# Five buffers for each split part of the weights, fewer raw buffers, and a tighter layout of all stages

## The chip, the cores and the metric

The kernel runs on one core of one Trainium2 chip. The metric is the device time of one execution in microseconds (us). Engines are named as in the profile: PE is TensorE's matmul side, PEld its weight loads, DVE is VectorE, ACT is ScalarE, POOL is GpSimd, SP is SyncE, whose queue issues most loads and stores.

## The reference, cut to what matters

One block of a network on 1,024 tokens of width 1,024, in float32: two branches (a gated MLP with causal mixing inside chunks of 128 tokens, and a state-space branch with a convolution and a scan over chunks), merged by gates, then a layer norm, then an expert layer that picks 128 of 16,384 experts per token.

```python
ya = gmlp_branch(uv, ...) @ gm_w_out
yb = ssd_branch(z, xbc, dt_raw, ...) @ ssd_w_out
merged = gates[..., 0, :] * ya + gates[..., 1, :] * yb
x1 = layer_norm(DEEPNORM_ALPHA * x + merged @ w_o, ...)
ch = peer(x1, ...)          # top 16 of 16x16 sums per head, 8 heads
ple = sigmoid(x1 @ ple_w_gate + ple_b_gate) * (p @ ple_w_proj)
x = layer_norm(DEEPNORM_ALPHA * x1 + ch + ple, ...)
# in peer, for the chosen experts eb and gates gb:
act = gelu(einsum('tkd,td->tk', u_tab[eb], xb))
out = einsum('tk,tkd->td', gb * act, v_tab[eb])
```

## The kernel before, in words

The tokens are worked in three groups of 2, 3 and 3 blocks of 128 (`GROUPS`, line 22). `front(gi)` runs the dense part of a group: the gated MLP (lines 239 to 350), the state-space branch (`conv`, `make_bc`, `make_x`, `core_g`, `core`, lines 364 to 507), the merge (509 to 527), the output product with the layer norm and the side product `ple` (530 to 645), and the scores for the experts (588 to 607). In the first two groups the chosen experts' rows are gathered by POOL (`gather`, line 800) and multiplied on DVE (`experts_u`, line 822) or on PE (`experts_v`, line 864); this gather work of a group runs beside the front of the later groups. The third group computes all experts densely (`dense_scores`, `dense_gates`, `dense`, lines 908 to 1020).

Every float32 product is made of three products of rounded halves (`mm3`, line 150). So each weight slice of 512 KB is loaded by SP into a buffer `raw`, cast by ACT into `whi` (line 146), and subtracted by DVE into `wlo` (line 147): a split. Then come 24 matmuls over it (18 in the second product of the dense stage). `weights` (line 138) holds 4 `raw`, 3 `whi` and 3 `wlo` buffers, which all weights share. The tokens xT are loaded and split in `prepare` (line 203) through 4 buffers of their own.

A scheduler sets the order on each engine: it takes the instructions in program order, by priority, and `tc.high_priority(offset=n)` moves what stands inside n places ahead. Each engine then works in that order and waits by semaphores for buffers and data.

In `dense`, `gte` (line 973) holds the gates for GI = 4 slices of 128 experts, read from DRAM in runs of GI*TC*4 = 512 bytes; `ewh`, `ewl` hold finished pieces, 13 of each. The output products land in 4 PSUM buffers `po`, of which a half step uses 3, and DVE adds them to `eacc` (line 1013).

```python
raw = wp.tile([128, k, n], F32, name="raw", tag="raw", bufs=4)
hi = wp.tile([128, k, n], F32R, name="whi", tag="whi", bufs=3)
lo = wp.tile([128, k, n], F32R, name="wlo", tag="wlo", bufs=3)
with tc.high_priority(offset=AHEAD_W[0]):
    DMA.dma_start(raw, src)
with tc.high_priority(offset=AHEAD_W[1]):
    A.copy(hi, raw)
    V.tensor_sub(lo, raw, hi.bitcast(F32))
```

Of the kernel before, what the change touches and what calls it, by code (L numbers as in the profile page):

```python
# [8 lines left out]
F32 = mybir.dt.float32  # L9
# [15 lines left out]
TC, GI = 32, 4  # L25
# [16 lines left out]
AHEAD_W = (20, 20)  # L42
# [36 lines left out]
def block_kernel(ctx, tc, a, out):  # L79
# [119 lines left out]
    def prepare(gi):  # L199
# [8 lines left out]
        with tc.tile_pool(name="xr", bufs=4, side=where) as xr:  # L208
            for k in range(KD):
                raw = xr.tile([128, T], F32, name="xraw")  # L210
                DMA.dma_start(raw, a["xT"][:, k, t0:t0 + T])
                split(xh[:, k], xl[:, k], raw)
        tokens[gi] = es, xp, xh, xl

    def front(gi):
# [24 lines left out]
        with tc.tile_pool(name="ga", bufs=1, side=side_) as ga, \  # L240
                tc.tile_pool(name="gb", bufs=2, side=side_) as gb:

            wst = ga.tile([128, 8, 128], F32, name="wst")
            DMA.dma_start(wst, a["wst"])
            add = ga.tile([128, 8, 128], F32, name="add")
            DMA.dma_start(add, rows(a["gmbs"], 0, 1024))
            V.tensor_mul(wst, wst, tri[:, None, :].to_broadcast([128, 8, 128]))
# [10 lines left out]
            with tc.tile_pool(name="sd", bufs=1, side=side_) as sd:  # L258
                raw = wp.tile([128, KD, NCOL], F32, name="raw", tag="raw", bufs=4)
                DMA.dma_start(raw, a["w_dt"])  # L260
                dh = wp.tile([128, KD, NCOL], F32R, name="whi", tag="whi", bufs=3)
                dl = wp.tile([128, KD, NCOL], F32R, name="wlo", tag="wlo", bufs=3)
                split(dh, dl, raw)
                pw = psm.tile([NCOL, T], F32, name="mm")
                for k in range(KD):
                    mm3(pw, (dh[:, k], dl[:, k]), (xh[:, k], xl[:, k]), k == 0, k == KD - 1)
                dtw = gb.tile([NCOL, T], F32, name="dtw", tag="t1", bufs=3)
                A.copy(dtw, pw)
                pd = pst.tile([128, NB, NCOL], F32, name="mt", tag="mt")
                for c in range(NB):  # L270
                    PE.transpose(pd[:, c, :], dtw[:, c * 128:c * 128 + 128], ident[:NCOL, :NCOL])
                sh = [128, NB, NCOL]
                dt = xp.tile(sh, F32, name="dt")
                V.tensor_add(dt, pd, dtb[:, None, :].to_broadcast(sh))
                e = sd.tile(sh, F32, name="e")
                A.activation(e, dt, AF.Abs)
                A.activation(e, e, AF.Exp, scale=-1.0)
                r = sd.tile(sh, F32, name="r")
                V.tensor_scalar_add(r, e, 2.0)
                V.reciprocal(r, r)  # L280
                V.tensor_mul(e, e, r)
                V.tensor_mul(r, e, e)
                q = sd.tile(sh, F32, name="q")
                V.tensor_scalar_mul(q, r, 2.0 / 17)
                for n in (15, 13, 11, 9, 7, 5, 3):
                    V.scalar_tensor_tensor(q, q, 2.0 / n, r, op0=OP.add, op1=OP.mult)
                V.scalar_tensor_tensor(q, q, 2.0, e, op0=OP.add, op1=OP.mult)
                V.scalar_tensor_tensor(dt, dt, 0.0, q, op0=OP.max, op1=OP.add)
                V.tensor_mul(e, dt, nega[:, None, :].to_broadcast(sh))
                pc = pst.tile([128, 2, NB * NCOL], F32, name="mt", tag="mt")  # L290
                dtaf = e.rearrange("p c h -> p (c h)")
                PE.matmul(pc[:, 0, :], lhsT=tri, rhs=dtaf, start=True, stop=True)
                PE.matmul(pc[:, 1, :], lhsT=ones, rhs=dtaf, start=True, stop=True)
                acs = xp.tile(sh, F32, name="acs")
                acsf = acs.rearrange("p c h -> p (c h)")
                A.copy(acsf, pc[:, 0, :])
                cdec = xp.tile(sh, F32, name="cdec")
                A.activation(cdec.rearrange("p c h -> p (c h)"), pc[:, 1, :], AF.Exp)
                dtd = xp.tile(sh, F32, name="dtd")
                dtdf = dtd.rearrange("p c h -> p (c h)")  # L300
                V.tensor_sub(dtdf, pc[:, 1, :], acsf)
                A.activation(dtdf, dtdf, AF.Exp)
                V.tensor_mul(dtd, dtd, dt)
                pt = pst.tile([NB * NCOL, 128], F32, name="mt", tag="mt")
# [4 lines left out]
                for c in range(NB):  # L309
                    DMA.dma_start(arow[:, c, :], act[c * NCOL:(c + 1) * NCOL, :])  # L310
# [809 lines left out]
```

## Time and profile before

| what | value |
|---|---|
| time, median of 3 runs | 3759.26 us (3750.78 to 3759.49) |
| the profiled execution's own time | 3774.55 us |
| its span, first to last instruction | 3772.9 us |
| PE busy | 3437.7 us, 91% |
| PEld busy | 2946.2 us, 78% |
| DVE busy | 2936.8 us, 78% |
| ACT busy | 1756.0 us, 47% |
| POOL busy | 1606.3 us, 43% |
| mean granted TensorE clock | 0.955 of full |
| moved by DMA | 1183.88 MB, mean 314 GB/s |

A share of busy time is an average over the whole span. A wait in the profile is an engine's idle time, put down to whatever ended it last. Matmuls follow each other before the one ahead has ended, so PE's busy time says when it had work, not how fast it went.

### The profile page before, as it was taken

What the parts mean: (1) busy time and instruction counts of PE and PEld (TensorE: products, weight loads), DVE (VectorE), ACT (ScalarE), POOL (GpSimd) and SP (SyncE); (2) the same over time, 40 slices, a digit from 0 to 9 for tenths busy, and PEclk for the clock granted to TensorE, in tenths of its full rate; (3) what the DMA queues carried; (4) which work ended last, traced back from release to release, by engine and by line L of the source; (5) the groups of instructions that cost most, each with busy time, mean ns of one, the idle gap of its engine ahead of it and who ended that gap; (6) DMA issues with size and microseconds to landing.
All of it is one profiled execution on the core that took longest, in us unless ns stands there. A gap on an engine that the chain in (4) does not pass through costs nothing.

```text
span 3772.9 us, 59493 instructions
## 1 busy us (share of the span) xinstructions
PE 3437.7 (91%) x21390; PEld 2946.2 (78%) x21390; DVE 2936.8 (78%) x6823; ACT 1756.0 (47%) x2675; POOL 1606.3 (43%) x1310
## 2 busy tenths in 40 slices
PE   8898997999989988999988989998889989989988
PEld 8897996988877876888878888777667868667756
DVE  6677799898977989896688999997667766766535
ACT  6788543476843333466652334774222323322223
POOL 0000004756545354554354445443556565665540
PEclk9998998999999988999989999999999999999999
DMA  5453656989879886989888899999999999999992
GB/s 200 161 172 130 238 180 241 389 309 356 317 279 385 309 324 234 356 311 343 305 326 327 298 338 349 362 377 372 360 381 400 395 386 389 368 383 401 356 350 95
DMA packets 409159, 1183.88 MB, mean 314 GB/s; under 512 B 41120, under 2 KB 139424, under 8 KB 405792
## 3 DMA queue, kind: packets, MB, share of 16 engines
q0 software_dynamic: 187488, 682.71, 47.7%
q1 hardware_dynamic: 221376, 497.38, 36.9%
q8 instruction: 168, 2.75, 0.3%
q14 instruction: 127, 1.04, 0.1%
HBM read 1121.01 MB, written 58.92 MB: 313 GB/s over the span
## 4 chain that ended last, share of the span: by engine, by line
PE 33%; DVE 16%; DMA 13%; issue 4%; ACT 1%; POOL 1%; SPq 0%; DVEq 0%; ACTq 0%; POOLq 0%
PE mm L152 6%; PE mm L154 6%; PE mm L153 6%; PE pacc L864 4%; DVE row L822 3%; DVE wlo L147 3%; DMA ew<-s 3%; PE po L152 3%; DMA row<-in_peer_v_dram,idxT 3%; PE po L153 3%; PE po L154 3%; DMA raw<-in_peer_uT_dram 2%; PE mt L947 2%; DMA row<-in_peer_u_dram,idx 1%; DMA raw<-in_peer_vd_dram 1%
## 5 line engine op out<-in xcount | busy, mean ns | idle before, releaser
L146 ACT CAST whi<-raw 128x1024 fp32r<-128x1024 f32 (+1 forms) x676 | 701.1, 1041 | 1192.4 <-PE mm L153 612.0
L803 POOL DMA_INDIRECT row<-in_peer_u_dram,idx x640 | 811.5, 1268 | 874.9 <-PE pacc L864 254.3
L147 DVE TENSOR_TENSOR wlo<-raw,whi 128x1024 fp32r<-128x1024 f32 (+1 forms) x676 | 816.2, 1210 | 375.5 <-ACT whi L146 374.7
L154 PE MATMUL mm<-xh,wlo 128*128 128x384 f32 (+2 forms) x3160 | 1056.4, 335 | 46.7 <-DVE wlo L147 46.7
L152 PE MATMUL mm<-xh,whi 128*128 128x384 f32 (+2 forms) x3160 | 1066.3, 338 | 34.3 <-ACT whi L146 25.6
L803 POOL DMA_INDIRECT row<-in_peer_v_dram,idxT x640 | 780.9, 1220 | 712.0 <-PE pacc L864 232.5
L153 PE MATMUL mm<-xl,whi 128*128 128x384 f32 (+2 forms) x3160 | 1051.9, 333 | 0.6 <-DVE xl L136 0.6
L822 DVE SCALAR_TENSOR_TENSOR row<-row,x1b 128x1024 f32<-128x1024 f32 x640 | 774.6, 1217 | 64.8 <-DMA row<-in_peer_u_dram,idx 58.5
L152 PEld LDWEIGHTS mm<-xh,whi 128*128 128x128 f32 (+1 forms) x3160 | 611.2, 194 | 89.7 <-ACT whi L146 46.1
L154 PEld LDWEIGHTS mm<-xh,wlo 128*128 128x128 f32 (+1 forms) x3160 | 609.8, 193 | 66.4 <-DVE wlo L147 55.0
L153 PEld LDWEIGHTS mm<-xl,whi 128*128 128x128 f32 (+1 forms) x3160 | 610.5, 193 | 12.2 <-issue 6.1
L864 PE MATMUL pacc<-row,zw 128*32 128x512 f32 x2560 | 316.9, 614 | 37.0 <-DMA row<-in_peer_v_dram,idxT 36.8
L152 PE MATMUL po<-whi,ewh 128*128 128x512 f32 x768 | 316.0, 411 | 32.2 <-DVE eacc L1013 32.2
L153 PE MATMUL po<-wlo,ewh 128*128 128x512 f32 x768 | 311.0, 405 | 14.4 <-DVE wlo L147 14.3
L154 PE MATMUL po<-whi,ewl 128*128 128x512 f32 x768 | 309.9, 404 | 0.0
L152 PEld LDWEIGHTS po<-whi,ewh 128*128 128x128 f32 x768 | 148.3, 193 | 104.6 <-DVE eacc L1013 36.1
L864 PEld LDWEIGHTS pacc<-row,zw 128*32 128x32 f32 x2560 | 67.9, 111 | 180.6 <-issue 131.1
L135 ACT CAST ewh<-ew 128x384 fp32r<-128x384 f32 x128 | 65.6, 514 | 296.7 <-DVE ew L985 230.1
L818 POOL DMA_DIRECT2D x1b<-x x5 | 3.0, 601 | 446.4 <-DMA x<-x 446.4
L153 PEld LDWEIGHTS po<-wlo,ewh 128*128 128x128 f32 x768 | 148.5, 193 | 51.0 <-DVE wlo L147 16.8
L154 PEld LDWEIGHTS po<-whi,ewl 128*128 128x128 f32 x768 | 148.1, 193 | 40.9 <-issue 5.0
L153 PE MATMUL mm<-wlo,xh 128*128 128x256 f32 x512 | 147.8, 289 | 11.4 <-DVE wlo L147 11.4
(272 smaller groups left out, 5603.8 us busy)
## 6 DMA issues: line engine op xcount, KB each, us to landing
raw<-in_peer_uT_dram SPq DMA_DIRECT2D x128, 512.0 KB, 8.0
raw<-in_peer_vd_dram SPq DMA_DIRECT2D x128, 512.0 KB, 6.8
raw<-in_w_xbc_dram SPq DMA_DIRECT2D x96, 512.0 KB, 5.9
raw<-in_w_g_dram SPq DMA_DIRECT2D x48, 512.0 KB, 6.7
raw<-in_w_z_dram SPq DMA_DIRECT2D x48, 512.0 KB, 5.4
raw<-in_ssd_w_out_dram SPq DMA_DIRECT2D x48, 512.0 KB, 5.3
raw<-in_w_q_dram SPq DMA_DIRECT2D x48, 512.0 KB, 4.7
g<-gt SPq DMA_DIRECT2D x24, 1024.0 KB, 7.5
```

Of the source, the lines that this page charges most:

```text
L135: A.copy(hi, src)
L146: A.copy(hi, raw)
L147: V.tensor_sub(lo, raw, hi.bitcast(F32))
L152: PE.matmul(p, lhsT=lh, rhs=rh, start=start, stop=False, skip_group_check=skip)
L153: PE.matmul(p, lhsT=lh, rhs=rl, start=False, stop=False, skip_group_check=skip)
L154: PE.matmul(p, lhsT=ll, rhs=rh, start=False, stop=stop, skip_group_check=skip)
L803: g = POOL.indirect_dma_start(out=t, out_offset=None, in_=a[tab], in_offset=bass.IndirectOffsetOnAxis(ap=ix, axis=0))
L818: POOL.dma_start(x1, x1_d[gi, c])
L822: u = V.scalar_tensor_tensor(t, t, 1.0, x1, op0=OP.mult, op1=OP.mult, accum_out=act[:, k:k + 1])
L864: return PE.matmul(pacc[q * 32:q * 32 + 32, h * 512:h * 512 + 512], lhsT=zws[z][:, q, r % 4, :], rhs=ts[q][:, h * 512:h * 512 + 512], star ...
L947: PE.matmul(p[:, i, :], lhsT=o1, rhs=o2, start=True, stop=True)
```

## The change

`weights` gets 3 `raw`, 5 `whi` and 5 `wlo` buffers, its loads stand 150 places ahead instead of 20, and its splits 100 instead of 20. The rest makes room in SBUF: GI is 2, so `gte` is loaded 64 times in runs of 256 bytes; the finished pieces are 11 of each; xT goes through the shared `raw` buffers, two rows of blocks at a time; the mixing weights `wst` and `add` are loaded and prepared per group g (`spatial`) instead of once; small tiles share the tag `t1`; `cT` has one buffer and `make_bc` stands after `core`; `ce` is written over `arow_t`, the square over `y`, the result of `ple` over `proj`; pT goes through a gather buffer, and its split (`ph`, `pl`) stands behind the output product. Besides, the adds to `eacc` stand 40 places ahead.

```diff
-TC, GI = 32, 4
+TC, GI = 32, 2
...
-AHEAD_W = (20, 20)
+AHEAD_W = (150, 100)
+NRAW, NHI = 3, 5
...
-        raw = wp.tile([128, k, n], F32, name="raw", tag="raw", bufs=4)
-        hi = wp.tile([128, k, n], F32R, name="whi", tag="whi", bufs=3)
-        lo = wp.tile([128, k, n], F32R, name="wlo", tag="wlo", bufs=3)
+        raw = wp.tile([128, k, n], F32, name="raw", tag="raw", bufs=NRAW)
+        hi = wp.tile([128, k, n], F32R, name="whi", tag="whi", bufs=NHI)
+        lo = wp.tile([128, k, n], F32R, name="wlo", tag="wlo", bufs=NHI)
...
-        with tc.tile_pool(name="xr", bufs=4, side=where) as xr:
-            for k in range(KD):
-                raw = xr.tile([128, T], F32, name="xraw")
-                DMA.dma_start(raw, a["xT"][:, k, t0:t0 + T])
-                split(xh[:, k], xl[:, k], raw)
+        for k in range(0, KD, 2):
+            raw = wp.tile([128, 2, T], F32, name="raw", tag="raw", bufs=NRAW)
+            DMA.dma_start(raw, a["xT"][:, k:k + 2, t0:t0 + T])
+            split(xh[:, k:k + 2], xl[:, k:k + 2], raw)
...
+            def spatial(g):
+
+                w = ws[g] = gb.tile([128, 128], F32, name="wst", bufs=3)
+                add = adds[g] = gb.tile([128, 1, 128], F32, name="add", bufs=3)
+                with tc.high_priority(offset=AHEAD_W[0]):
+                    DMA.dma_start(w, a["wst"][:, g, :])
+                    DMA.dma_start(add[:, 0], rows(a["gmbs"], g * 128, 128))
+                V.tensor_mul(w, w, tri)
+                pr = pst.tile([128, 128], F32, name="mt", tag="mt")
+                PE.matmul(pr, lhsT=ones, rhs=w, start=True, stop=True)
+                V.scalar_tensor_tensor(add[:, 0], pr, gmb[:, g:g + 1], add[:, 0], op0=OP.mult, op1=OP.add)
...
-                xc = sb.tile([128, T], F32, name=name, bufs=1 if name == "bT" else 2)
+                xc = sb.tile([128, T], F32, name=name, bufs=2 if name == "xs" else 1)
...
-                if j % 2 == 1 and j < 15:
-                    yield from make_bc(j // 2 + 1)
                 if j < 15:
                     yield from make_x(j + 1)
                 if j % 2 == 0:
                     core_g(j // 2)
                 yield from core(j)
+                if j % 2 == 1 and j < 15:
+                    yield from make_bc(j // 2 + 1)
...
-            if u == 1:
-                split(ph, pl, pT)
             yield 2 * unit
         mp_es.close()
+        lp = qa_es.enter_context(tc.tile_pool(name="lp", bufs=1, side=side_))
+        ph = lp.tile([128, 2, T], F32R, name="ph")
+        pl = lp.tile([128, 2, T], F32R, name="pl")
+        split(ph, pl, pT)
...
-                ready[i2] = [eb.tile([128, T], F32R, name=n, bufs=I2B + 5) for n in ("ewh", "ewl")]
+                ready[i2] = [eb.tile([128, T], F32R, name=n, bufs=I2B + 3) for n in ("ewh", "ewl")]
...
-                        V.tensor_add(o, o, po[c])
+                        with tc.high_priority(offset=AHEAD_G):
+                            V.tensor_add(o, o, po[c])
```

The change moves instructions on every engine. Three places are shown. In a row, a line number is that of its own file, and the number in a tile's name tells one buffer use from another; a slice's cast, as `whi_7761`, and the product made with it, as `mm_7766`, lie 5 apart.

ACT, in the gated MLP of the second group, where the gates `sg` are taken from the products `mm`. Before, from the product with `whi_7679` on (the next slices in order of use are 7712, 7761, 7794, 7840, 7873):

```order
L146 CAST whi_7794<-raw_7793 128x1024
L344 ACT_TABLE_LOAD
L344 ACTIVATE sg_7709<-mm_7684,c_bgate_121 128x384
L146 CAST whi_7840<-raw_7839 128x1024
L146 CAST whi_7873<-raw_7872 128x1024
L344 ACTIVATE sg_7791<-mm_7766,c_bgate_121 128x384
```

Now, from the product with `whi_7693` on (the next slices are 7726, 7775, 7808, 7854, 7887, 7936, 7969, 8015):

```order
L147 CAST whi_7854<-raw_7853 128x1024
L750 COPY gate0_1_7633<-pr_7611 128x128
L346 ACT_TABLE_LOAD
L346 ACTIVATE sg_7723<-mm_7698,c_bgate_121 128x384
L147 CAST whi_7887<-raw_7886 128x1024
L136 CAST gh_7063<-mix_7681 128x384
L346 ACTIVATE sg_7805<-mm_7780,c_bgate_121 128x384
L147 CAST whi_7936<-raw_7935 128x1024
L147 CAST whi_7969<-raw_7968 128x1024
L147 CAST whi_8015<-raw_8014 128x1024
L346 ACTIVATE sg_7884<-mm_7859,c_bgate_121 128x384
```

When the first of these gates is taken, three casts of later slices stood ahead of it before, and four now.

SP, at the start of the kernel. Before (with the semaphores that a row waits for):

```order
1 L211 DMA xraw_150<-in_xT_dram 128x256
...
4 L211 DMA xraw_162<-in_xT_dram 128x256
5 L144 DMA raw_203<-in_w_v_dram 128x1024
6 L144 DMA raw_233<-in_w_v_dram 128x1024
7 L211 DMA xraw_166<-in_xT_dram 128x256 [waits DMAHW0_49,DVE_49]
```

Now:

```order
1 L211 DMA raw_147<-in_xT_dram 128x2x256
...
3 L211 DMA raw_155<-in_xT_dram 128x2x256
4 L313 DMA wst_523<-in_wst_dram 128x128
...
9 L314 DMA add_583<-in_gmbs_dram 128x128 [waits DMAHW0_49]
10 L211 DMA raw_159<-in_xT_dram 128x2x256 [waits DMAHW1_49,DVE_49]
11 L145 DMA raw_178<-in_w_v_dram 128x1024 [waits DMAHW2_49,DVE_49]
12 L145 DMA raw_208<-in_w_v_dram 128x1024 [waits DMAHW3_49,DVE_49]
```

The first load of weights waited for nothing before; now it stands behind all of xT and waits until DVE has split the second pair of its rows.

ACT, at the end of the merge of the second group (the casts `mh` are the merge's last results, those of 128x512 belong to `ple_w_proj`). Before:

```order
L135 CAST mh_11955<-ya_12597 128x384
L146 CAST whi_12865<-raw_12864 128x1024
L146 CAST whi_12926<-raw_12925 128x1024
L135 CAST ph_12705<-pT_12700 128x768
L146 CAST whi_12968<-raw_12967 128x1024
```

Now:

```order
L136 CAST mh_11938<-ya_12580 128x384
L147 CAST whi_12945<-raw_12944 128x1024
L147 CAST whi_13014<-raw_13013 128x1024
L147 CAST whi_13056<-raw_13055 128x1024
L147 CAST whi_13165<-raw_13164 128x512
L147 CAST whi_13196<-raw_13195 128x512
L147 CAST whi_13226<-raw_13225 128x512
L147 CAST whi_13257<-raw_13256 128x512
L136 CAST ph_13124<-row_12898 128x768
```

The cast `ph` stood in the middle of the casts for the output product before; now it stands behind the casts of the four slices that are multiplied with it.

## Rows read from the trace of the kernel before

**Rows 1.** The page, part 1: busy us, share of the span, instructions of each engine.

```profile
PE 3437.7 (91%) x21390; PEld 2946.2 (78%) x21390; DVE 2936.8 (78%) x6823; ACT 1756.0 (47%) x2675; POOL 1606.3 (43%) x1310
```

**Rows 2.** Waits of PE, whole span: waiter <- releaser: us in total, times, longest.

```profile
PE mm L154 <- DVE wlo L147: 46.7, 28, 8.5
PE mm L152 <- ACT whi L146: 39.5, 29, 8.4
PE pacc L864 <- DMA row<-in_peer_v_dram,idxT: 36.8, 13, 8.4
PE po L152 <- DVE eacc L1013: 32.2, 7, 13.5
...
PE mm L153 <- DVE wlo L147: 23.5, 9, 6.2
PE po L153 <- DVE wlo L147: 14.3, 5, 5.2
```

**Rows 3.** Windows: start:end us, PE, PEld, DVE, ACT, POOL busy, PEclk, DMA share, GB/s.

```profile
0.00:560.00 560.00, 511.70 (x4040) 491.20 (x4041) 411.27 (x1041) 381.08 (x615) 2.17 (x9) 0.95 0.53 180
560.00:735.00 175.00, 148.48 (x809) 140.69 (x808) 163.15 (x379) 61.65 (x85) 105.32 (x72) 0.92 0.81 304
735.00:1215.00 480.00, 446.28 (x2979) 393.20 (x2978) 402.76 (x762) 290.77 (x450) 251.41 (x188) 0.97 0.89 329
1215.00:1505.00 290.00, 251.81 (x1601) 215.65 (x1602) 264.24 (x944) 101.14 (x148) 130.64 (x103) 0.92 0.81 292
1505.00:2080.00 575.00, 535.35 (x3499) 472.67 (x3497) 462.00 (x842) 307.20 (x476) 275.67 (x228) 0.96 0.90 328
2080.00:2600.00 520.00, 482.04 (x3050) 417.38 (x3049) 507.59 (x1740) 282.06 (x461) 239.35 (x204) 0.98 0.92 347
2600.00:3640.00 1040.00, 952.42 (x4883) 726.19 (x4881) 663.55 (x1037) 291.10 (x393) 594.59 (x500) 0.96 1.01 382
```

**Rows 4.** Timeline of PE in the state-space branch: start us, us, operation; 18 matmuls apart.

```profile
1699.82 0.33 PE L152 MATMUL mm<-xh,whi 128*128 128x384 f32 x1
...
1702.94 0.33 PE L152 MATMUL mm<-xh,whi 128*128 128x384 f32 x1
```

**Rows 5.** Waits of PE for splits, windows 560:735, 1215:1505 and 2080:2600 us.

```profile
PE mm L154 <- DVE wlo L147: 13.4, 4, 8.5
...
PE mm L152 <- ACT whi L146: 3.9, 5, 1.0
...
PE mm L153 <- DVE wlo L147: 8.5, 2, 5.4
...
PE mm L152 <- ACT whi L146: 6.4, 6, 1.9
PE mm L154 <- DVE wlo L147: 4.6, 5, 1.3
...
PE mm L154 <- DVE wlo L147: 18.5, 13, 5.7
...
PE mm L152 <- ACT whi L146: 4.8, 7, 1.4
...
PE mm L153 <- DVE wlo L147: 2.1, 2, 1.1
```

**Rows 6.** DMA of the dense stage, 2680:3600 us: queues (packets, MB, share), one issue.

```profile
q0 software_dynamic: 64658, 235.46, 65.3%
q1 hardware_dynamic: 69428, 116.35, 35.1%
...
gte<-g SPq DMA_DIRECT2D x26, 768.0 KB, 15.2
```

**Rows 7.** Timeline of the start: start us, us, operation [idle before <-releaser].

```profile
2.67 0.91 SPq L144 DMA_DIRECT2D raw<-in_w_v_dram  x2
...
7.29 1.04 ACT L146 CAST whi<-raw 128x1024 fp32r<-128x1024 f32 x1 [2.53 <-DMA raw<-in_w_v_dram]
...
8.38 0.58 PE L152 MATMUL mm<-whi,xh 128*128 128x256 f32 x1 [8.38 <-ACT whi L146]
```

More of the change, by code (lines that the diff above doesn't have):

```diff
@@ L256, in front @@
                 yield 2 * unit
[L258 to L304, printed above, removed]
-                PE.transpose(pt, acsf, ident)
-                act = sd.tile([NB * NCOL, 128], F32, name="q")
-                A.copy(act, pt)
-                arow = dram.tile([NCOL, NB, 128], F32, name=f"arow{gi}")
-                for c in range(NB):
-                    DMA.dma_start(arow[:, c, :], act[c * NCOL:(c + 1) * NCOL, :])
@@ new lines, in front @@
+            raw = wp.tile([128, KD, NCOL], F32, name="raw", tag="raw", bufs=NRAW)
+            DMA.dma_start(raw, a["w_dt"])
+            dh = wp.tile([128, KD, NCOL], F32R, name="whi", tag="whi", bufs=NHI)
+            dl = wp.tile([128, KD, NCOL], F32R, name="wlo", tag="wlo", bufs=NHI)
+            split(dh, dl, raw)
+            pw = psm.tile([NCOL, T], F32, name="mm")
+            for k in range(KD):
+                mm3(pw, (dh[:, k], dl[:, k]), (xh[:, k], xl[:, k]), k == 0, k == KD - 1)
+            dtw = gb.tile([NCOL, T], F32, name="dtw", tag="t1", bufs=3)
@@ new lines, in front @@
+            A.copy(dtw, pw)
+            pd = pst.tile([128, NB, NCOL], F32, name="mt", tag="mt")
+            for c in range(NB):
+                PE.transpose(pd[:, c, :], dtw[:, c * 128:c * 128 + 128], ident[:NCOL, :NCOL])
+            sh = [128, NB, NCOL]
+            dt = xp.tile(sh, F32, name="dt")
+            V.tensor_add(dt, pd, dtb[:, None, :].to_broadcast(sh))
+            erq = gb.tile([128, T], F32, name="erq", tag="t1", bufs=3)
+            e, r, q = [erq[:, n * NB * NCOL:(n + 1) * NB * NCOL].rearrange("p (c h) -> p c h", c=NB) for n in range(3)]
@@ new lines, in front @@
+            A.activation(e, dt, AF.Abs)
+            A.activation(e, e, AF.Exp, scale=-1.0)
+            V.tensor_scalar_add(r, e, 2.0)
+            V.reciprocal(r, r)
+            V.tensor_mul(e, e, r)
+            V.tensor_mul(r, e, e)
+            V.tensor_scalar_mul(q, r, 2.0 / 17)
+            for n in (15, 13, 11, 9, 7, 5, 3):
+                V.scalar_tensor_tensor(q, q, 2.0 / n, r, op0=OP.add, op1=OP.mult)
+            V.scalar_tensor_tensor(q, q, 2.0, e, op0=OP.add, op1=OP.mult)
+            V.scalar_tensor_tensor(dt, dt, 0.0, q, op0=OP.max, op1=OP.add)
@@ new lines, in front @@
+            V.tensor_mul(e, dt, nega[:, None, :].to_broadcast(sh))
+            pc = pst.tile([128, 2, NB * NCOL], F32, name="mt", tag="mt")
+            dtaf = e.rearrange("p c h -> p (c h)")
+            PE.matmul(pc[:, 0, :], lhsT=tri, rhs=dtaf, start=True, stop=True)
+            PE.matmul(pc[:, 1, :], lhsT=ones, rhs=dtaf, start=True, stop=True)
+            acs = xp.tile(sh, F32, name="acs")
+            acsf = acs.rearrange("p c h -> p (c h)")
+            A.copy(acsf, pc[:, 0, :])
+            cdec = xp.tile(sh, F32, name="cdec")
@@ L312, in front @@
+            A.copy(act, pt)
+            arow = dram.tile([NCOL, NB, 128], F32, name=f"arow{gi}")
+            for c in range(NB):
+                DMA.dma_start(arow[:, c, :], act[c * NCOL:(c + 1) * NCOL, :])
             for c in range(NB):
                 normalize(v[:, c], st[:, c], gb)
-            for g4 in range(0, 8, 4):
-                pr = pst.tile([128, 4, 128], F32, name="mt", tag="mt")
-                PE.matmul(pr.rearrange("p g t -> p (g t)"), lhsT=ones,
-                          rhs=wst[:, g4:g4 + 4].rearrange("p g t -> p (g t)"), start=True, stop=True)
-                for g in range(g4, g4 + 4):
-                    V.scalar_tensor_tensor(add[:, g], pr[:, g - g4], gmb[:, g:g + 1], add[:, g],
-                                           op0=OP.mult, op1=OP.add)
+            ws, adds = {}, {}
@@ L424, in core @@
                 A.activation(dec, dec, AF.Exp, scale=-1.0)
[L425 removed]
+                ce = arow_t
                 A.activation(ce, arow_t, AF.Exp)
@@ L587, in front @@
             for u in range(16):
+                if u == 4:
+                    plb = lg
+                    DMA.dma_start(plb, rows(a["ple_b_gate"], 0, 1024))
                 p = channel_major(a["w_q"][u], xh, xl)
```

57 lines of the change are left out of this document (31 added, 26 removed).

## The prediction

> **What bounds the kernel now.** I read the page first. PE is the busiest engine, 3437.7 of 3772.9 us [rows 1], so the gain to be had is in the 335 us in which it was idle and in the time at a lower clock. Then I read who PE waited for. Splits of weights end 46.7 + 39.5 + 23.5 + 14.3 = 124.0 us of it, gathered rows 36.8 us, the adds to `eacc` 32.2 us [rows 2]. Of the first four rows one is of the dense stage alone: 14.3 us at `po`. So a third of PE's idle time hangs on the part that the change enlarges.
>
> Then the windows, because what a wait is worth depends on its stage [rows 3]. The reader should look at three columns. Where DVE has room (0 to 560, 735 to 1215, 1505 to 2080: 411 of 560, 403 of 480, 462 of 575 us), a split that is late is late by its place in the queue. In three windows DVE is nearly full (560 to 735, 1215 to 1505, 2080 to 2600): it is idle for 11.9 + 25.8 + 12.4 = 50.0 us of 985, and a split is late there because DVE has too much to do. From 2600 to 3640 the DMA share is 1.01: there the queue of loads has no room left.
>
> The granted clock is the last column read. It has two levels, 1.2 and 2.4 GHz, so a mean of 0.95 is 10% of the window at the lower one. Over the six windows before 2600 that is 56 + 28 + 29 + 46 + 46 + 21 = 226 us at 1.2 GHz, beside 224 us of idle PE (the windows less PE's busy time: 48 + 27 + 34 + 38 + 40 + 38). At half speed at most half of 226 us is lost, and in part of it PE had nothing to do; I take half of that half, 56 us. So each us of PE's waiting costs some 0.25 us more by the clock, and I multiply a wait that goes by 1.25.
>
> **The change part by part.** All sums are against the profiled execution's own 3774.55 us, which is 15 us over the median of the runs; the difference is then taken from the median, 3759.26 us.
>
> *Five split buffers, splits 100 places ahead.* The 18 matmuls between the two rows of [rows 4] take 3.12 us, 0.173 us each, so a slice of 24 is 4.2 us of PE. With three buffers the cast of slice n waits until PE has done with slice n-3; then two slices lie before its use, 8.3 us. With five it waits for n-5, and four slices lie before, 16.7 us. In the built order this holds: at ACT's gates four casts stand ahead instead of three, and over all 679 splits the number of matmuls between release and use has a median of about 95 instead of 50. A cast takes 1.04 us [rows 7] and the subtraction about as long (estimate). So what can delay a split without a stall grows from some 6 to some 14 us, more than the longest of these waits, 8.5 us [rows 2].
>
> Free windows: the 124.0 us less 62.2 us in the full windows (the sum of [rows 5]) and less 14.3 us in the dense stage leave 47.5 us; 8.4 us of them are the first wait of the kernel [rows 7] and stay. Of 39.1 us I take three quarters, 29, because a core step that PE waits for can now stand behind an earlier split; with the clock **-37 us** (bounds 0 and -49).
>
> Full windows: 62.2 us hang on splits. DVE's work in them does not change, and two more split buffers let it do only two splits beforehand, about 2.5 us per window. PE can then catch up only as far as DVE was idle, 50.0 us. I take a third, 17, with the clock **-21 us** (bounds 0 and -62). The rest of these waits will appear under another name: DVE's selection, its gather products or its norms.
>
> *Dense stage: splits and the adds 40 places ahead.* They end 14.3 + 32.2 = 46.5 us of waits [rows 2]. The DMA share is 1.01 here [rows 3], so PE made faster only waits for loads. I take a quarter, **-12 us** (bounds 0 and -58, with the clock).
>
> *GI = 2: runs of 256 bytes.* The bytes stay, the packets of `gte` double. The price is read from the queues [rows 6]: q0 moves gathered rows of 4 KB, 65.3% of 920 us for 235.46 MB, 2.55 us per MB. On q1 the 168 weight slices (88.1 MB) at that rate would take 225 of its 323 us (35.1%), which leaves 98 us for the other 28.3 MB, of which `gte` is 20.4. At the rate of q0 these would take 72. The 26 us more, put on the 26 loads of `gte`, make 1.0 us for each. If that is a fixed time per packet, twice as many packets cost 1.0 us more for each of the 32 loads before, 32 us; the lower bound is 0. If a packet of 256 bytes takes as long as one of 512, each 768 KB take 3.0 us more (20.4 MB at 2.55 is 52, with the 26 that is 78, over 26): 96 us. I take the fixed time, the nearest row, and half of it, as PE and DMA take turns as the bound in this stage: **+16 us** (0 to +96).
>
> The Trainium skill speaks against this part: "DMA: Bandwidth & Descriptors", section Specifications, asks for transfers of at least 512 B for line rate and says that below it the engine reads, modifies and writes. No row here has such runs in a loaded queue. By that page the term would be the upper bound, and the sum would be 80 us worse.
>
> *Three raw buffers.* A load can be issued once the split three slices earlier is done instead of four, one slice, 4.2 us, later against its cast. If it is late, ACT and then DVE stand behind it, but PE has four slices in hand. I cost it at 0 in the sum; the cover is the split buffers, and without it each late load costs what it is late.
>
> *Start.* The first load of weights went out at 2.67 us and its product began at 8.38 [rows 7]. Now it waits for the second pair of xT rows and stands behind ten more issues, which I put at 2 to 5 us: **+3 us**.
>
> *The cast `ph`.* It now stands directly ahead of its product in the second and third group, so PE waits there for a cast and a subtraction of 768 columns, under 1.04 us [rows 7] each: **+4 us** (0 to 4.2, less the earlier waits there).
>
> *The mixing weights in pieces.* Eight small masks and products per group for one and two large ones, 42 more small loads, behind which SP's loads stand: **+3 us** (0 to 8), on DVE in its full windows. `make_bc` after `core` with one `cT`: the same instructions, less distance from the convolution to `core_g`, more from `core` to the next; 0 (-6 to +6). The merged xT loads, `ce`, `sq` and `proj` in place, `ple`'s single buffer: 0, off the path or only tighter.
>
> Sum: -37 - 21 - 12 + 16 + 3 + 4 + 3 = **-44 us**, 3759.26 - 44 = **3715 us**.
>
> **The rivals.**
>
> *PE is freed almost everywhere.* For it: DVE's idle time would cover 50 us even in the full windows, and a fuller reserve may smooth the dense stage too. Against it: DMA at 1.01. Then 39.1 + 50.0 + 46.5 = 136 us go, with the clock 170, less 26 us of costs: 144 us faster, 3615 us. Chance 0.12 for anything beyond 85 us faster.
>
> *The waits change their names.* The splits run ahead only where ACT and SP let them: with three raw buffers and a full DVE the fifth buffer stays empty, so the change would not do what it says where it matters. Then the free windows give half (-20, with the clock -25), the others nothing, and the costs of 26 us eat it: about 3760 us. For it: the full windows, 985 us long. Chance 0.15 for within 11 us.
>
> *The small runs of `gte` win.* Place: the dense stage, where the queue is full. Price: up to +96 us there, with -70 and +10 from the rest +36 us, 3795 us. It decides from about 1.9 us more for each 768 KB on (60 us over 32 loads), between the 1.0 of a fixed time and the 3.0 of the upper bound. For it: the DMA share of 1.01. Against it: already at 512 bytes the trace shows only 1.0 us over the rate of q0. The Trainium skill's rule above ("DMA: Bandwidth & Descriptors", Specifications) names this mechanism. Chance 0.17, other slips included.
>
> **How the numbers follow.** The forecast, 15 to 85 us faster, has 0.56. A measurement of this kernel can tell about 0.3%, 11 us, from no change. Faster takes the forecast and the first rival, 0.68; no change 0.15; slower 0.17. The range leaves out the far half of the first rival and of the last: 3650 to 3780 us.
>
> **What would show it right or wrong.** Right: PE's waits for `whi` and `wlo` fall from 124 us to under 55, nearly to nothing outside the full windows and the start; in the full windows DVE comes closer to 100% and PE's waits for other DVE results stay or grow; the window from the first `peer_vd` load to the last gather is about as long as before, its `gte` loads carry a larger share per MB; the first matmul begins near 11 us. Wrong: waits for splits that stay where DVE has room, a dense stage longer by over 40 us (then the small runs), one shorter by over 40 (then DMA was not the bound), or new waits of PE behind casts that wait for raw loads.

## The result and the profile after

The changed kernel takes 3890.61 us (median of 4 runs, 3879.06 to 3901.14), the kernel before 3759.38 on the same chip: ratio 1.0351, 95% interval 1.0314 to 1.0387, 131 us slower. I had forecast 44 us faster. The profiled execution has a span of 3899.4 us, 126.5 more than before. The page, part 1, as in [rows 1]:

```profile
PE 3465.0 (89%) x21426; PEld 2964.3 (76%) x21426; DVE 2937.0 (75%) x6832; ACT 1748.5 (45%) x2658; POOL 1578.5 (40%) x1310
```

DVE's work is the same to 0.2 us. PE's idle time (span less busy) grew from 335.2 to 434.4 us, by 99, and its busy time by 27: the mean granted clock fell from 0.955 to 0.941. So the loss begins with waiting, and in this trace PE's busy time grew by 0.28 us for each us of it, at the lower clock. Who PE waited for, as in [rows 2]:

```profile
PE po L153 <- DVE eacc L1020: 81.9, 13, 15.9
PE mm L153 <- ACT whi L147: 45.3, 13, 15.3
PE pacc L870 <- DMA row<-in_peer_v_dram,idxT: 36.4, 11, 10.9
PE mm L155 <- DVE wlo L148: 21.5, 21, 2.9
```

The waits for `wlo`, 84.5 us in all in [rows 2], fell to 22.6 (with 1.1 in a row not shown), those for `whi` stayed at some 40 us (45.3 after 39.5). What is new is one step back: whom ACT waited for with its casts (the same view of ACT; the first four weights by size).

```profile
ACT whi L147 <- DMA raw<-in_peer_vd_dram: 200.6, 44, 16.0
...
ACT whi L147 <- DMA raw<-in_peer_uT_dram: 118.0, 44, 10.9
...
ACT whi L147 <- DMA raw<-in_gm_w_out_dram: 67.5, 15, 11.2
ACT whi L147 <- DMA raw<-in_ple_w_gate_dram: 52.4, 19, 10.8
```

Summed over all weights, ACT stood still for `raw` loads 202 times, 654.5 us. In the trace of before the same sum is 32 times, 140.3 us. Two stretches of the timeline show what this does. First ACT at the end of the third group's output product (start us, us, operation, [idle before <- releaser]):

```profile
2053.51 1.14 ACT L147 CAST whi<-raw 128x512 fp32r<-128x512 f32 x2 [9.88 <-DMA raw<-in_ple_w_proj_dram]
2060.84 0.62 ACT L147 CAST whi<-raw 128x512 fp32r<-128x512 f32 x1 [6.18 <-DMA raw<-in_ple_w_proj_dram]
2068.86 0.62 ACT L147 CAST whi<-raw 128x512 fp32r<-128x512 f32 x1 [7.40 <-DMA raw<-in_ple_w_proj_dram]
2069.39 0.83 ACT L136 CAST ph<-row 128x768 fp32r<-128x768 f32 x1
```

and PE there:

```profile
2070.26 0.58 PE L153 MATMUL mm<-whi,ph 128*128 128x256 f32 x1 [6.65 <-ACT ph L136]
```

These are the four casts that the built order showed ahead of `ph`. The fourth needs a fourth `raw` buffer, which isn't there: it waits 7.40 us for its load, `ph` stands behind it, and PE waits for `ph`. The second stretch, among the scores, ACT and then PE:

```profile
2183.33 0.48 ACT L603 COPY sk<-mt 128x384 f32<-128x384 f32 x1 [1.07 <-PE mt L600]
2191.12 1.04 ACT L147 CAST whi<-raw 128x1024 fp32r<-128x1024 f32 x1 [7.31 <-DMA raw<-in_ple_w_gate_dram]
2192.07 0.47 ACT L597 COPY qT<-mm 128x384 f32<-128x384 f32 x1
```

```profile
2187.10 0.34 PE L153 MATMUL mm<-xh,whi 128*128 128x384 f32 x1
2192.60 0.80 PE L600 MATMUL mt<-kT,qT 128*128 128x128 f32 x2 [5.16 <-ACT qT L597]
```

PE was done with the product at 2187.4. The copy `qT` of 0.47 us could have followed, but it stood behind a cast for a slice that is wanted several slices later and whose load had not landed. The Trainium skill says that ScalarE's and VectorE's queues are strict FIFO ("PSUM — Partial Sum Buffer", Engine vs sequencer instructions); the trace agrees.

The windows at the old times (columns as in [rows 3]) show where:

```profile
2080.00:2600.00 520.00, 448.21 (x2731) 384.20 (x2729) 456.77 (x1549) 243.49 (x395) 210.61 (x181) 0.93 0.83 305
2600.00:3640.00 1040.00, 917.17 (x4709) 712.77 (x4710) 679.44 (x1167) 306.70 (x433) 578.56 (x472) 0.94 1.00 366
```

From 2080 to 2600 DVE was not fuller than before but emptier: 456.8 us instead of 507.6 [rows 3], with PE at 448 instead of 482 and the DMA share at 0.83 instead of 0.92. The changed kernel is later there, so the two windows hold other work. Taken between the same products (the fifth and sixth column of the window table further down), the stretch takes 572 us instead of 519, and DVE is busy for 506 and 507 us of it: the same work, spread over more time.

### The profile page after: what moved, and what is told of

Its sections match the earlier page's. It is cut to its first block, busy times and chain, and to the rows that moved or that the text cites. A ratio compares the mean times of both kernels' runs of the same rounds, so it can differ in the third digit from the quotient of the medians.

```text
span 3899.4 us, 59692 instructions
## 1 busy us (share of the span) xinstructions
PE 3465.0 (89%) x21426; PEld 2964.3 (76%) x21426; DVE 2937.0 (75%) x6832; ACT 1748.5 (45%) x2658; POOL 1578.5 (40%) x1310
## 5 line engine op out<-in xcount | busy, mean ns | idle before, releaser
L809 POOL DMA_INDIRECT row<-in_peer_u_dram,idx x640 | 792.6, 1238 | 959.7 <-DVE row L828 348.4
L809 POOL DMA_INDIRECT row<-in_peer_v_dram,idxT x640 | 772.0, 1206 | 792.5 <-DVE row L828 248.9
L155 PE MATMUL mm<-xh,wlo 128*128 128x384 f32 (+2 forms) x3160 | 1060.7, 336 | 20.5 <-DVE wlo L148 20.5
L153 PE MATMUL po<-whi,ewh 128*128 128x512 f32 x768 | 317.5, 413 | 81.9 <-DVE eacc L1020 81.9
L870 PE MATMUL pacc<-row,zw 128*32 128x512 f32 x2560 | 324.1, 626 | 36.7 <-DMA row<-in_peer_v_dram,idxT 36.4
L991 DVE TENSOR_TENSOR ew<-ew,gte 128x384 f32<-128x384 f32 x128 | 71.1, 558 | 171.1 <-DMA ew<-s 88.4
```

The lines of the kernel that those rows point to most:

```text
L153: PE.matmul(p, lhsT=lh, rhs=rh, start=start, stop=False, skip_group_check=skip)
L155: PE.matmul(p, lhsT=ll, rhs=rh, start=False, stop=stop, skip_group_check=skip)
L809: g = POOL.indirect_dma_start(out=t, out_offset=None, in_=a[tab], in_offset=bass.IndirectOffsetOnAxis(ap=ix, axis=0))
L870: return PE.matmul(pacc[q * 32:q * 32 + 32, h * 512:h * 512 + 512], lhsT=zws[z][:, q, r % 4, :], rhs=ts[q][:, h * 512:h * 512 + 512], star ...
L991: V.tensor_mul(w3, w3, gte[0][:, :, i2 % GI, :])
```

## The experiments

The kernels ran on several chips, on which the kernel before takes 3784 to 3794 us instead of 3759. So times are compared as ratios to the kernel before on the same chip; its trace was taken there once more. "Raw, split" is NRAW, NHI; "waits" is the sum over all weights of ACT's waits for `raw` loads, us and times.

| run | raw, split | ratio (95% interval) | waits |
|---|---|---|---|
| before, again | 4, 3 | 1 | 101, 25 |
| e10 before, 150/100 ahead | 4, 3 | 0.9989 (0.9965 to 1.0012) | 97, 21 |
| e16 before, ahead in free stages | 4, 3 | 0.9980 (0.9966 to 0.9995) | 102, 26 |
| e4 before, GI = 2 | 4, 3 | 1.0052 (1.0029 to 1.0074) | 166, 37 |
| e11 change, GI = 4 | 5, 4 | 1.0028 (1.0015 to 1.0041) | 46, 17 |
| e12 change, GI = 4, splits 20 ahead | 5, 4 | 1.0049 (1.0032 to 1.0066) | 61, 22 |
| e3 change | 5, 4 | 1.0072 (1.0053 to 1.0090) | 75, 23 |
| e7 change, adds back | 5, 4 | 1.0089 (1.0062 to 1.0116) | 75, 21 |
| e1 change, old depth | 4, 3 | 1.0082 (1.0062 to 1.0101) | 179, 42 |
| e6 change | 4, 4 | 1.0118 (1.0094 to 1.0142) | 211, 61 |
| e15 change, 3 whi, 5 wlo | 3, 3/5 | 1.0160 (1.0140 to 1.0180) | 342, 90 |
| e9 change | 3, 3 | 1.0177 (1.0160 to 1.0195) | 360, 95 |
| e5 before, 3 raw | 3, 3 | 1.0189 (1.0157 to 1.0222) | 388, 103 |
| e13 change | 3, 4 | 1.0249 (1.0228 to 1.0271) | 514, 140 |
| the change | 3, 5 | 1.0351 (1.0314 to 1.0387) | 655, 202 |
| e2 change, 20/20 ahead | 3, 5 | 1.0470 (1.0441 to 1.0498) | 798, 245 |
| e14 change, 5 whi, 3 wlo | 3, 5/3 | 1.0657 (1.0627 to 1.0686) | 1446, 447 |

From some 340 us on, the loss rises with ACT's waits for loads. Below that it does not follow them: there the layout and the small runs set it.

To see where time is lost I counted the weight products (the matmuls of `mm3`, 16,008 in every trace) and took the start of some of them, in us:

| product | 1,200 | 3,600 | 7,200 | 8,400 | 10,800 | 12,000 | 15,600 |
|---|---|---|---|---|---|---|---|
| before, first trace | 191 | 563 | 1394 | 1706 | 2270 | 2665 | 3667 |
| the change | 182 | 560 | 1418 | 1725 | 2298 | 2743 | 3793 |
| before, again (e8) | 190 | 560 | 1402 | 1711 | 2274 | 2685 | 3682 |
| e4 GI = 2 | 190 | 561 | 1397 | 1707 | 2274 | 2692 | 3710 |
| e1 old depth | 190 | 567 | 1417 | 1724 | 2286 | 2700 | 3714 |
| e3 5 raw, 4 split | 178 | 549 | 1387 | 1707 | 2266 | 2693 | 3708 |
| e10 before, ahead | 172 | 560 | 1387 | 1693 | 2255 | 2679 | 3674 |
| e11 5 raw, 4 split, GI = 4 | 177 | 549 | 1385 | 1704 | 2255 | 2679 | 3683 |
| e12 as e11, splits 20 ahead | 189 | 563 | 1401 | 1728 | 2287 | 2699 | 3686 |

The first two rows are of one chip, the others of slower ones. Each row is one trace: e4, whose first half is that of before, is up to 5 us from e8 by product 10,800, so differences of that size there tell nothing.

**The first set: which part of the change.** e1 takes the depth back, e2 the places ahead alone, e3 moves one buffer of each split part to `raw`, e4 is the kernel before with the small runs.

```diff
e1
-AHEAD_W = (150, 100)
-NRAW, NHI = 3, 5
+AHEAD_W = (20, 20)
+NRAW, NHI = 4, 3
...
-                        with tc.high_priority(offset=AHEAD_G):
-                            V.tensor_add(o, o, po[c])
+                        V.tensor_add(o, o, po[c])
```

> The changed layout with the old depth: 4 raw and 3 whi/wlo buffers, loads and splits 20 places ahead, adds to eacc not ahead; GI = 2 and all the rest as changed. Theory A (the 131 us are lost because casts placed far ahead wait on ACT for loads that three raw buffers let out late, and what stands behind them on ACT and DVE waits too): most comes back, 3770 to 3810 us, ACT's waits for raw loads fall from some 650 us to under 300. Theory B (the 256-byte runs fill the loaded queue): 3830 us or more, the dense stage as long as in the changed kernel. Theory C (the tighter layout itself: make_bc after core, one cT, mixing weights in pieces): 3860 us or more, and the fronts stay slow.

```diff
e2
-AHEAD_W = (150, 100)
+AHEAD_W = (20, 20)
```

> The changed kernel with one edit: AHEAD_W = (20, 20), so 3 raw and 5 whi/wlo buffers stay. Theory A: part comes back, 3810 to 3860 us, since three raw buffers still hold loads back but fewer casts stand ahead of other work. Theory D (the place in the order alone does the harm, whatever the buffers): nearly all comes back, 3760 to 3790 us. Theory B or C: no change, 3880 to 3900 us.

```diff
e3
-NRAW, NHI = 3, 5
+NRAW, NHI = 5, 4
```

> The changed kernel with one edit: NRAW, NHI = 5, 4, so the same room goes to raw buffers; AHEAD_W stays (150, 100). Theory A: more than half comes back, 3770 to 3820 us, ACT's waits for raw loads fall to under a third of the changed kernel's some 650 us. Theory D: little comes back, 3860 us or more. Theory B: the dense stage stays as long as in the changed kernel (within 15 us).

```diff
e4, in the kernel before
-TC, GI = 32, 4
+TC, GI = 32, 2
```

> The kernel before with one edit: GI = 2, so gte is loaded 64 times in runs of 256 bytes. In the trace of the changed kernel the packets of 256 bytes took 118 us of 16 engines in all; 49,152 packets of 512 bytes at the 29 ns of before would be 89 us, so 29 us more. Theory A: 10 to 35 us slower than before, 3770 to 3795 us. Theory B: 60 us slower or more, 3820 us and above.

Theory B falls by e4 (1.0052) and C by e1 (1.0082). e3 gives most of the loss back with one edit, 2.8%, and ACT's waits for loads fall from 655 to 75 us. In e3 PE's waits for `whi` and `wlo` are 36.6 us in all, where before, taken again, has 129.0; that is what I had hoped for, and still e3 is slower than before, by 0.7%, of which the small runs explain 0.5: PE is idle for 370.4 us instead of 342.8, above all by `eacc` (80.9 after 20.8) and `ew` (20.5 after 5.8). D falls by e2, which no theory had right: with the splits back at their old place the kernel is slower still, 1.0470. A part of that can be read from the trace. I paired each load, cast and subtraction by their order. From a cast's start to its subtraction's end are 6.53 us in e2 and 6.15 in the changed kernel, in the fourth eighth of the slices 8.29 and 6.70 (means): a subtraction further ahead on DVE frees its `raw` buffer sooner. That this is worth the 1.2% between the two kernels is not shown.

The same pairing shows why `raw` is the narrow place. In every trace the load goes out 0.03 to 0.06 us (median) after the subtraction that frees its buffer, so a buffer is never free for long. Between the load's issue and its cast lie 16.3 us with four buffers (before, again) and 10.4 us with three (the changed kernel; means). The load itself takes 4.4 to 7.2 us to land (list of issues on the page of the changed kernel, by weight). What a load may be late fell from some 10 us to some 4 (estimate, the first less the second).

The trace of e4 prices the small runs, in 2700 to 3620 us, beside before on a like chip (packets, MB, share). Before, again:

```profile
q1 hardware_dynamic: 68896, 115.87, 35.0%
...
gte<-g SPq DMA_DIRECT2D x26, 768.0 KB
```

e4:

```profile
q1 hardware_dynamic: 108784, 115.38, 37.4%
...
gte<-g SPq DMA_DIRECT2D x50, 384.0 KB
```

2.4% of 920 us are 22 us more on this queue, and from product 12,000 to 15,600 e4 takes 1018 us, before 997: 21 us. A packet of 512 bytes took 27 ns and one of 256 bytes 18 (medians over each trace): twice as many cost 9 ns more per 512 bytes, not 27.

**The second set: `raw` alone, the other buffers, the adds.**

```diff
e5, in the kernel before
-        raw = wp.tile([128, k, n], F32, name="raw", tag="raw", bufs=4)
+        raw = wp.tile([128, k, n], F32, name="raw", tag="raw", bufs=3)
```

> The kernel before with one edit: 3 raw buffers instead of 4, everything else as before. Theory A (sharpened by the first runs: every load goes out within about 0.03 us of the split that frees its buffer, so the raw buffers are the pipe of the weights; a slice holds its buffer for the load, some 6.5 us, and for cast and subtraction, 5 to 13 us, and three buffers leave no slack): 70 to 150 us slower than before, ratio 1.02 to 1.04, ACT's waits for raw loads from 140 us to above 500. Rival E (three buffers hurt only together with casts far ahead or with the tighter layout): within 30 us of before, ratio under 1.008.

```diff
e6
-NRAW, NHI = 3, 5
+NRAW, NHI = 4, 4
```

> The changed kernel with one edit: NRAW, NHI = 4, 4, loads and splits 150 and 100 places ahead. Theory A: close to the run with five raw and four split buffers, ratio 1.005 to 1.018; if what lies ahead counts as the sum of raw and split buffers (8 here, 8 in the changed kernel, 9 in the run with 5 and 4, 7 before), the result stays at 1.03 or above.

```diff
e7: as e3, and
-                        with tc.high_priority(offset=AHEAD_G):
-                            V.tensor_add(o, o, po[c])
+                        V.tensor_add(o, o, po[c])
```

> The changed kernel with NRAW, NHI = 5, 4 and the adds to eacc back at their own place (no 40 places ahead). If the adds ahead help, as the prediction had it: 5 to 20 us slower than the run with 5 and 4 alone, ratio 1.010 or more. If they only rename the wait, ratio 1.006 to 1.009. If they harm, because an add ahead of its product's end holds up DVE, and PE's wait for eacc went from 32 to 81 us for that reason: 1.004 or less, and PE's wait for eacc under 50 us.

> The kernel before, unchanged, for its trace on the chip on which the other runs of this set are made: by all theories the waits and stage lengths of the first trace, apart from what this chip does more slowly.

e5 alone costs 1.9%, just under the range that theory A expected, with 388 us of waits instead of over 500. So one `raw` buffer fewer costs some 71 us with nothing else changed. e6 and e3 have 8 and 9 buffers and the changed kernel 8: it isn't their sum that counts. e7 does not decide between "rename" and "help": its interval holds e3's ratio, and PE's wait for `eacc` is 76.6 us against 80.9 in e3. The adds' place does not set that wait. e8 had nothing new to tell, and serves as the base of the tables.

**The third set: the split buffers beside three `raw`, and what is left to gain.**

```diff
e9
-NRAW, NHI = 3, 5
+NRAW, NHI = 3, 3
```

> The changed kernel with two buffers fewer for each split part: NRAW, NHI = 3, 3, loads and splits still 150 and 100 places ahead. Theory A in its strong form (with three raw buffers the fourth and fifth split buffers hardly ever fill, so they bring nothing): within 0.5% of the changed kernel, ratio 1.030 to 1.042. If more split buffers let casts stand further ahead of ACT's other work and so make the shortage of raw buffers worse: 1.020 to 1.028, about the sum of the layout with the old depth (1.0082) and of three raw buffers (1.0189). If the reserve of split buffers covers late loads, as the prediction had it: 1.045 or more.

```diff
e10, in the kernel before
-AHEAD_W = (20, 20)
+AHEAD_W = (150, 100)
```

> The kernel before with one edit: AHEAD_W = (150, 100), with its 4 raw and 3 split buffers. If the place in the order is what loses time in the windows where DVE is full (splits ahead of results that PE waits for sooner): slower by 0.3 to 1.5%, the loss between the scores of a group and the start of the next. If the buffers set how far a split runs ahead, and the place only says who goes first among ready ones: within 0.3%. A gain of over 0.3% would say that the place alone is worth having.

```diff
e11
-TC, GI = 32, 2
+TC, GI = 32, 4
...
-NRAW, NHI = 3, 5
+NRAW, NHI = 5, 4
...
-                ready[i2] = [eb.tile([128, T], F32R, name=n, bufs=I2B + 3) for n in ("ewh", "ewl")]
+                ready[i2] = [eb.tile([128, T], F32R, name=n, bufs=I2B + 1) for n in ("ewh", "ewl")]
```

> The changed kernel with NRAW, NHI = 5, 4, GI = 4 again, and 9 finished pieces ewh and ewl instead of 11 for the room. If the costs add: 1.0072 of the run with 5 and 4 less the 0.0052 of the small runs, 0.999 to 1.005. If the dense stage needs the finished pieces that are given up: 1.007 or more.

```diff
e12: as e11, and
-AHEAD_W = (150, 100)
+AHEAD_W = (150, 20)
```

> As the run before it (5 raw, 4 split buffers, GI = 4, 9 finished pieces), with AHEAD_W = (150, 20): loads far ahead, splits at the place of the kernel before. If the place of the splits is what loses time in the windows where DVE is full: 0.990 to 0.999, faster than with 100. If the buffers alone set the lead: equal to the run with 100 within 0.3%. If splits at 20 give up the gain in the first front too: 1.003 to 1.010.

e9 was the surprise: with two split buffers fewer the changed kernel is 1.7% faster, 1.0177, below even the range given for harm. The strong form of A, that the fourth and fifth buffer bring nothing, falls; they do harm. e10 is the change's idea at no cost in room, and it moves the end by nothing that can be told (0.9989). Its trace says why: 15 us ahead at product 7,200, 19 at 10,800, and from there to 12,000 it takes 424 us where before takes 411. Its waits say more: `whi` and `wlo` together fall from 129.0 to 60.5 us, and PE is idle as long as before, 341.3 and 342.8 us, because others grew: `dec` from 23.7 to 44.2, `xl` from 3.2 to 20.7, `eacc` from 20.8 to 32.0, `xh` from 0 to 10.2. e11 adds up as expected. e12 is no faster (the third of its cases), but its trace moves the loss: 412 us from 10,800 to 12,000, where e11 takes 424, and no gain by product 1,200 (189 us, e11 177).

**The fourth set: casts or subtractions.**

```diff
e13
-NRAW, NHI = 3, 5
+NRAW, NHI = 3, 4
```

> The changed kernel with NRAW, NHI = 3, 4. Theory A2 (more split than raw buffers: a burst of casts, up to as many as there are split buffers, finds only as many loads as there are raw buffers, and ACT stands still for a load with other work behind it): between the runs with 3 and 5 split buffers, ratio 1.021 to 1.031, and ACT's waits for raw loads between their 360 and 655 us. If the harm has another cause in the fifth buffer (its room, its place): 1.015 to 1.021.

```diff
e14
-        lo = wp.tile([128, k, n], F32R, name="wlo", tag="wlo", bufs=NHI)
+        lo = wp.tile([128, k, n], F32R, name="wlo", tag="wlo", bufs=3)
```

> The changed kernel with 5 whi, but 3 wlo buffers; 3 raw buffers stay. If the casts on ACT do the harm (they run ahead alone): 1.027 or more. If the raw buffer's life does it: a subtraction that waits for a wlo buffer now holds the raw buffer longer, so fewer loads go out, yet casts can't run ahead of loads either; then about as the run with 3 and 3, 1.014 to 1.022.

```diff
e15
-        hi = wp.tile([128, k, n], F32R, name="whi", tag="whi", bufs=NHI)
+        hi = wp.tile([128, k, n], F32R, name="whi", tag="whi", bufs=3)
```

> The changed kernel with 3 whi and 5 wlo buffers; 3 raw buffers stay. By theory A2 the casts are held by the 3 whi buffers, so as the run with 3 and 3: 1.014 to 1.022. If the subtractions on DVE, put further ahead, do the harm: 1.027 or more.

```diff
e16, in the kernel before
-AHEAD_W = (20, 20)
+AHEAD_W = (150, 100)
...
-    def weights(src, k, n):
+    def weights(src, k, n, ahead=AHEAD_W):
...
-        with tc.high_priority(offset=AHEAD_W[0]):
+        with tc.high_priority(offset=ahead[0]):
...
-        with tc.high_priority(offset=AHEAD_W[1]):
+        with tc.high_priority(offset=ahead[1]):
...
-            p = channel_major(a["peer_uT"][i2], xh, xl)
+            p = channel_major(a["peer_uT"][i2], xh, xl, (20, 20))
```

> The kernel before with loads and splits 150 and 100 places ahead in the stages where DVE has room (w_v, w_u, w_g, gm_w_out, ssd_w_out, w_o, ple_w_proj, w_q, ple_w_gate), and still 20 and 20 for w_xbc, w_z, peer_uT and peer_vd; buffers as before, 4 raw and 3 split. In the trace with all weights ahead PE was 18 us further after the first 1,200 weight products and up to 24 us further later on, and lost some 15 us in the first core steps and 13 us where DVE works at the scores. If both add: 10 to 25 us faster than before, ratio 0.993 to 0.998. If what is gained is lost at the next full stage anyway: 0.998 to 1.002.

e13 lies between e9 and the change, e15 on e9, and e14 beyond all: theory A2 stands. It is the `whi` buffers that let casts stand further ahead on ACT than loads can come: e15 takes two of them away, leaves `wlo` at five, and has the time of e9. e14 alone would not show it, as a second cause comes in there: the casts run ahead of `wlo` too, and a subtraction that waits for a `wlo` buffer holds its `raw` buffer meanwhile (10.05 us from cast to subtraction's end, 4.85 in e9; means).

What the fourth and fifth split buffer do to PE is read from the change beside e9. They do shorten the waits for splits: `whi` and `wlo` cost PE 67.9 us instead of 109.3. But what stands behind the casts costs more: `eacc` 81.9 after 47.1, `ew` 27.0 after 10.3, `btok` 11.6 after 3.8, `qT` 14.1 after 7.0, `ph` 6.7 after nothing. PE is idle for 434.4 us instead of 389.1. e9's rows for this:

```profile
PE po L153 <- DVE eacc L1020: 47.1, 8, 16.0
PE mm L153 <- ACT whi L147: 41.6, 19, 12.1
...
PE mm L153 <- ACT ew L989: 10.3, 2, 9.2
```

Beside e3, whose loads come in time, the change loses elsewhere: `whi` itself costs PE 45.3 us after 13.9, gathered rows 36.4 after 18.7, `o` 15.4 after 7.2. `eacc`, `ew` and `qT` are high in e3 too (80.9, 20.5 and 13.9), so these follow how far the splits run ahead more than whether the loads are late.

ACT in e9, its two largest waits for loads:

```profile
ACT whi L147 <- DMA raw<-in_peer_vd_dram: 184.9, 29, 18.5
...
ACT whi L147 <- DMA raw<-in_peer_uT_dram: 56.1, 22, 12.3
```

in e14:

```profile
ACT whi L147 <- DMA raw<-in_peer_vd_dram: 554.1, 108, 19.6
ACT whi L147 <- DMA raw<-in_peer_uT_dram: 253.3, 84, 17.1
```

e16 is the one version whose interval lies below 1, by 0.20% (0.05 to 0.34), some 7 us; that is less than the 0.3% I set as the bound of what can be told, and on the edge of both cases expected: most of what is gained in one stage is lost in the next.

## Why the prediction was wrong

The loss adds up from the ratios: small runs 0.52% (e4), the rest of the layout 0.30% (e1 less e4; their intervals overlap), three `raw` buffers 0.95% (e9 less e1, with the places ahead), two more split buffers beside them 1.74% (the change less e9). In us some 20, 11, 36 and 66. The shares hold for this order of the steps only: three buffers alone cost 71 us (e5), and the step from e1 to e9 also holds what the places ahead bring. My costs of 26 us for the layout and the small runs were near the 31 measured. What was wrong is 102 us for the buffers, which I had at 0, and 70 us of gain that did not come.

- **The step that failed** is "*Three raw buffers* ... I cost it at 0 in the sum; the cover is the split buffers". The split buffers cover only the waits for the splits themselves (41 us fewer than in e9); for what stands behind the casts on ACT they are the other side of the shortage. A reserve behind a cast fills only as fast as loads come, and I counted what it could hold (four slices, 16.7 us of PE), not what three loads could bring. Alone the step costs 71 us (e5), in this layout 36, and with the five buffers that were to cover it another 66. I had seen that "ACT and then DVE stand behind it" and did not ask what else stands there: `ew`, `btok`, `qT`, `ph`, each a step that PE waits for. The last line of my own list, new waits behind casts that wait for loads, is what came.
- **Free windows, -37, and full windows, -21.** The other way round, and together nothing. The windows of [rows 3], taken between the products that begin them in the first trace (3,579, 4,322, 6,312, 7,536, 9,960, 11,745), in us:

| run | free | full | free | full | free | full | sum of free | sum of full |
|---|---|---|---|---|---|---|---|---|
| before, first trace | 560 | 182 | 476 | 287 | 576 | 519 | 1612 | 988 |
| the change | 557 | 166 | 506 | 287 | 585 | 572 | 1648 | 1025 |
| before, again (e8) | 558 | 187 | 478 | 290 | 573 | 533 | 1609 | 1010 |
| e4 GI = 2 | 559 | 185 | 477 | 288 | 575 | 541 | 1611 | 1014 |
| e10 before, ahead | 558 | 169 | 486 | 272 | 591 | 529 | 1635 | 970 |
| e3 5 raw, 4 split | 546 | 169 | 500 | 280 | 581 | 546 | 1627 | 995 |
| e12 splits 20 ahead | 561 | 181 | 484 | 297 | 575 | 535 | 1620 | 1013 |

  With enough `raw` buffers and splits 100 places ahead (e10, e3) the full windows are 15 to 40 us shorter, about as forecast, and the free ones 18 to 26 us longer, where I had 37 shorter; only in the first of them e3 gains 12. The step that failed here is "DVE's work in them does not change". Beside before, taken again, DVE is busy in the full windows for 912 us in both instead of 940, and in the second and third free window for 890 instead of 861: some 28 us of its work were put off from a full window to the free one behind it, where PE's idle time rose from 66 us to 88. With splits at 20 (e12) DVE is busy for 938 us in the full windows, nearly as before. In the change the shortage of loads comes on top of this, above all in the third full window.

  The last of the gain is lost at the end of the third full window and the start of the dense stage. From product 10,800 to 12,000 before takes 411 us, e4 418, e3 427, e10 424, and with splits at 20 (e12) 412. e3's waits of PE from 2266 to 2693 us, the stretch between these products:

```profile
PE mm L153 <- ACT ew L989: 15.5, 2, 8.3
...
PE mm L155 <- DVE wlo L148: 5.8, 9, 1.8
```

  In the same stretch of before, taken again, `whi` and `wlo` cost PE 11.3 us, `sah` 6.4 and `ew` 2.2; in e3 `sah` costs 1.4. Some 10 us of waits for splits and `sah` went and 13 for `ew` came.

- **Dense stage, -12.** It came to nothing. The waits for `wlo` at `po` are gone and those for `eacc` grew from 32 to 82 us: a new name. The adds' own place is not the reason (e7). e3 takes as long there as the small runs alone would explain (1015 us from 12,000 to 15,600, e4 1018).
- **GI = 2, +16.** Right: 20 us (11 to 28), between my fixed time of 32 and its half. By the two medians a packet has a fixed part of 9 ns (estimate); 96 packets of 512 bytes for each load and DMA engine make 0.9 us of it, where I had 1.0. The Trainium skill's rule of 512 bytes ("DMA: Bandwidth & Descriptors", Specifications), read as I read it, would have given 96 us, and the measurement decides against that: 36 ns for 512 bytes in two packets, not 54.
- **Start, +3.** 4.4 us: the first load of weights goes out at 5.78 us and the first product begins at 12.75; they were at 2.67 and 8.38 [rows 7].

```profile
5.78 6.31 SPq L145 DMA_DIRECT2D raw<-in_w_v_dram  x3
...
12.75 0.58 PE L153 MATMUL mm<-whi,xh 128*128 128x256 f32 x1 [12.75 <-ACT whi L147]
```

- **The cast `ph`, +4.** 10.0 us (6.7 for `ph` in the third group, where the casts ahead of it wait, and 3.3 for `pl`); the built order shown ahead of the prediction had told which. But e3, where loads come in time, has 10.1 as well (2.8 and 7.3): its new place costs that much without the shortage.
- **Mixing weights +3, `make_bc` 0.** PE waits 7.5 us for the masks and, over the whole span, 31.5 for `bT`, `cT` and `btok` of the state-space branch (2.1 for `btok` before). In e1, with the old places, only 3.1 and 2.6 are left; in e3, with splits 100 places ahead and loads in time, 7.0 and 23.6. So most of this comes from the splits' place ahead of these steps, not from late loads.
- **The clock, 1.25 per us.** 1.28 in this trace, which is partly luck: beside before, taken again, PE's busy time grew by 0.13 us per us of idle time in e9, 0.33 in e14 and 0.57 in e5. No single factor is shown.

Of the rivals, "waits change their names" had the mechanism nearest to it (three `raw` buffers hold the splits back, and waits come back under other names) and stopped at no gain. The slower rival was of the right sign by the wrong place.

Open is why e2 is as slow as it is beyond what the subtractions' place explains, and how much of PE's 99 us passes through each follower on ACT. The idle times of both engines laid over each other give a part: in the change PE stood still for 61 us while ACT stood still for a `raw` load, in before for 26, in e3 for 5. The rest of the loss reaches PE later, and its way is not shown.

## What to carry to other kernels

In this chain of load, cast and use the room belonged first to the loads (5 raw and 4 split buffers 1.0072, 3 and 5 of them 1.0351). A cast placed ahead of its load blocks everything behind it on ACT, which worked in order; so here the finished halves should have had no more buffers than there were raw ones (three raw with 3, 4 and 5 halves: 1.0177, 1.0249, 1.0351). Holding the casts back by the order did not help (e2). Before adding depth, look at what an engine's waits are at the step before the one that is late, and try the place in the order first: e10 took half of the waits for splits away without any room, and showed at the same time that the kernel was no faster for it. A wait that goes is a gain only if the work that was put off for it is not waited for in the next stage.

## What I had not expected of the hardware

Halving a run of 512 bytes costs 9 ns, not another 27: a packet of 256 bytes took 18 ns, in e4's dense stage with this queue at 37.4% and all DMA engines busy. And a program with nearly the same work on every engine (DVE 2936.8 and 2937.0 us, ACT 1756.0 and 1748.5) ran 126 us longer: 99 us are waits of PE, and 27 are its own work, which took longer at a lower mean granted clock, 0.941 after 0.955.
